# One layer of a hybrid SSD and convolution backbone: a new table of issue orders for the five engines

## The chip, the cores and the metric

The kernel runs on one core of a Trainium2 chip. The metric is the device time of one execution in microseconds (us). Five engines matter: TensorE (PE) does the matmuls, VectorE (DVE), ScalarE (ACT) and GpSimd (POOL) work on tiles element by element, and SyncE (SP) issues the DMAs. Each engine works through its own list of instructions in order; an instruction whose operand is not there yet holds up all that stands behind it on that engine.

## The reference

One layer of a diffusion backbone, for 512 latent tokens and 128 context tokens (640 columns in all, written T here), model width 1024. Cut to what matters:

```python
mod = silu(cond) @ w_ada + b_ada                      # six vectors of 1024, for latent and context
sh1, sc1, g1, sh2, sc2, g2 = split(mod, 6)
h = rms_norm(x, norm_mix_pre) * (1 + sc1) + sh1
z, xbc, dt_raw, cf_in = split(h @ w_in)
xbc = silu(dwconv1d(xbc, w_ssd_conv))                 # width 3
xs, b_mat, c_mat = split(xbc)
y_f, s_f = ssd_chunked(xs, dt_f, a_f, b_mat, c_mat, init_f)     # Mamba-2, chunks of 128, 16 heads
y_b, s_b = ssd_chunked(flip(xs), flip(dt_b), a_b, ...)          # and backward
y_ssd = rms_norm((y_f + flip(y_b) + xs * d_skip) * silu(z), ssd_norm)
u = cf_a * sigmoid(cf_g)                              # from cf_in
u = silu(layer_norm(dwconv1d(u, w_cf_conv)))          # width 31
mix = concat([y_ssd, u]) @ w_out
x = x + g1 * rms_norm(mix, norm_mix_post)
h = rms_norm(x, norm_ffn_pre) * (1 + sc2) + sh2
up = dwconv(h @ w_ffn_up)                             # 3x3 on latent tokens, width 3 on context
f = (silu(gate) * val) @ w_ffn_down                   # 2816 wide
x = x + g2 * rms_norm(f, norm_ffn_post)
```

Outputs are the new tokens and the final SSD states of the context. All is in float32.

## The kernel before

**Products.** Every tile has 128 channels on the partitions and the 640 tokens along the free axis. A float32 product is made as three products of reduced float32 (fp32r): weight and activation are split into a high part and the rest (hi and lo), and `mm3` (L408 to L414) adds hi·hi, hi·lo and lo·hi in PSUM, in two column halves of 384 and 256. A weight block of 128 by 1024 is called a unit: `fetch` (L286) has SP load it into `wr` (two buffers), `split_unit` (L290 to L312) has ACT copy the high part into `wh` (L310) and POOL (a few times DVE) subtract it to get `wl` (L312), three buffers each. Activations are split by `split_act` (L399, L401).

**Stages.** The times are those of the profile before.

- 0 to 36 us: x is loaded, squared on ACT (L497) and summed over channels on PE (L472, a product with ones, as every sum over channels); `rsqrt_mean` makes the root on ACT (L486) and its reciprocal on DVE (L487); `spread` (L480) brings it to all partitions. The first adaLN vectors are made by `ada_first` in four stages (L440 products of 16 loaded tiles, ACT copy L443, transpose L422, DVE L431), x is modulated (L522 to L533) and split, and the first three units run as the rows of h become ready. L506 is the product for dt.
- 36 to 340 us: projections, units 3 to 35, with eight pairs of heads p = 0 to 7 of the SSD between them. L657 to L664 prepare the decays. For each pair: transposes to tokens (L591), weighting by POOL (L729), chunk states (L743, L745) copied from PSUM by ACT (L747), the scan over chunks by POOL (L755, L758), state products y_off (L806, scaled by DVE L808), and the products within chunks y_diag (L817). The width-31 convolution runs on DVE (L871), some of its taps on ACT and POOL (L880, L884); ACT L851 is the gate's tanh.
- 340 to 400 us: the sums of the layer norm, the high and low parts of the first five SSD rows (L997 on DVE), the layer norm itself (DVE L980, ACT L984, DVE or POOL L985). Units 36 to 43, "ahead" parts of the output projection (the five SSD rows that need no layer norm), run beside it.
- 400 to 480 us: the rest of the output projection, units 44 to 58, and between its parts the remaining adaLN vectors, `ada_half` 0 to 5 (L459 products of eight tiles that SP has loaded into slots that the layer norm and the splits have read; then L462, L422).
- 480 to 535 us: class `Mid`, once for each column half: sum of squares and root, `spread`, `x2` (DVE L1155, L1157, ACT square L1158), `xsum` (L472), root, `spread`, and h2. Beside it units 59 to 64, the first up-projection units (L1258) and the last adaLN half, 6.
- From 535 us on: up-projections with the 3x3 convolution on DVE (L1236), down-projections, and the output.

**Order.** The program text makes the instructions in plain order; what is issued when is written out by hand in the table `ORDER`: for each engine the full sequence (PE 6677 entries, DVE 1076, ACT 785, POOL 412, SP 360) as ranges of program indices. `issue_in_order`, called at the end, ties each instruction to the one before it in that list, without a semaphore:

```python
for e, text in ORDER.items():
    order = []
    for word in text.split():
        a, _, b = word.partition("-")
        order += range(int(a), int(b or a) + 1)
    for a, b in zip(order, order[1:]):
        tc.add_manual_dep(given[e][b], given[e][a].name, behind, reason="order")
```

The buffers that an instruction uses and the data it waits for are fixed by the program text; the table sets only when it is issued on its engine.

Of the kernel before, what the change touches and what calls it, by code (L numbers as in the profile page):

```python
# [50 lines left out]
0-27 36-45 28-31 46-50 32-34 51-67 35 68-70 102 71-80 103 81-100 116-118 101 104-111 119-121 112-114 122  # L51
173-174 140-172 115 175-181 123-127 187-192 128-129 193-197 130-131 182-186 132-134 244-245 211-242 198
246-247 258-260 248-251 243 252 261-267 135-137 253 138-139 199-200 268-269 254-255 201-204 256-257 205-210
284-287 296-297 288-293 270 282-283 320-327 271-275 294-295 298 276 299-307 277 341 278-281 308-319 342-388
399-421 328-332 422-488 495-497 489-494 498-514 543-551 515-530 552-562 531-534 563-565 535-542 566-581
645-646 582-587 647-651 588 652-656 333-335 657-659 589-590 336-340 389-393 660-694 394-398 695-713 741-745
714-730 746-754 731-739 755-758 595 591-594 759-768 740 769-776 789-801 777-778 802-806 779-785 807-820
786-788 821-836 600-603 596-599 604-608 878-945 613-616 609-612 621-624 617-620 641-644 625-640 946-960
974-982 961 983-985 962 837-841 963 986 964-973 987-1018 1022-1023 1019-1021 1024-1033 846-849 842-845
854-857 850-853 1034-1043 1070-1078 1044-1058 1079-1084 1059-1069 1085-1107 1118-1129 1108-1117 1130 858-877  # L60
1131-1162 1207-1223 1163-1165 1224-1253 1255 1254 1256-1284 1303-1314 1285-1302 1315-1332 1351-1354
1333-1347 1166-1170 1355-1360 1348-1350 1361-1379 1450-1456 1380-1381 1457-1476 1382-1398 1175-1178
1171-1174 1183-1186 1179-1182 1203-1206 1187-1202 1477-1499 1399-1403 1500-1571 1594 1572-1589 1595-1601
1590-1593 1602-1608 1404-1408 1609-1622 1683 1623-1641 1409-1416 1421-1423 1417-1420 1424 1684-1715
1425-1437 1441-1444 1438-1440 1731-1746 1445-1449 1747-1755 1716-1720 1756-1758 1721-1724 1642-1646
# [12 lines left out]
2802-2809 2842 2854 2897-2901 2855-2860 2927-2930 2861-2873 2902-2924 2960-2962 2925-2926 2931-2935
2874-2886 2936-2938 2887-2892 2939-2958 2893 2959 3092-3093 2963-2975 3026 2976-2990 3027-3038 2991-2992
3039 3059-3070 2993-2998 3071 2999 3072-3073 3000-3016 3074-3077 3017-3024 3078-3090 3040-3044 3094-3096  # L80
3045-3058 3025 3097-3139 3158-3160 3140-3147 3161 3148-3157 3162 3203-3209 3163-3171 3210-3211 3172-3175
3184-3198 3212-3220 3301 3176-3183 3302-3306 3236 3199-3202 3091 3221-3235 3237-3245 3307-3310 3246-3253
3270 3311-3314 3271-3273 3315 3274 3316-3317 3275-3284 3318-3327 3332-3348 3254-3269 3285-3300 3328-3331
3380-3383 3349-3373 3388-3390 3397-3399 3410 3384-3387 3374-3376 3391-3393 3400-3402 3413-3415 3411
3406-3409 3539-3570 3412 3419 3422-3423 3420 3377-3379 3394-3395 3424 3431-3433 3440-3442 3449-3451 3421
3428-3430 3437-3439 3446-3447 3396 3403-3405 3448 3416-3417 3515-3517 3418 3518-3530 3425-3426 3531-3535
3455-3470 3477-3492 3471-3473 3536 3474-3476 3493-3499 3537 3427 3434-3436 3505-3508 3500-3504 3509-3514
3538 3443-3445 3452-3454 3572-3575 3644-3647 3668-3669 3576-3578 3648-3650 3670-3674 3579-3581 3571
3651-3653 3582-3584 3654-3656 3675-3680 3585-3587 3657-3659 3681-3682 3620-3623 3588-3590 3624-3625
# [12 lines left out]
419 395-400 420 428 401-403 432 463 404 464 405 465 442-443 406 421 423 444 424-425 407-409 422 445 410-412
# [1493 lines left out]
```

## Time and profile before

| | |
|---|---|
| median of 3 runs | 988.61 us (986.96 to 988.88) |
| the profiled execution | 989.1 us, of which the span 987.1 us |
| mean granted clock of PE over the span | 0.991 |
| busy: PE, DVE, ACT, POOL | 950.4, 690.3, 473.3, 577.1 us |
| moved by DMA | 117.52 MB, 119 GB/s on average |

The span runs from the first to the last instruction of the profiled execution; its time has 2.0 us besides. A row of the timeline reads: start in us, duration in us, engine, source line, operation, output <- input by the program's names, shape, type and count of instructions put together, and in brackets how long the engine had been idle before it and what it waited for. A row of the windows reads: stretch, its length, then for each engine the busy time and the count, then the mean granted clock of PE (1 is full speed), the busy share of the DMA engines and their GB/s.

### The profile page before, as it was taken

The page shows a single profiled execution, that of the slowest core. Times are in us where ns is not written, and L with a number is a line of the kernel's source. Part 1 is how long each engine was busy: PE and PEld are TensorE (multiplying, and loading weights), DVE is VectorE, ACT ScalarE, POOL GpSimd, SP SyncE. Part 2 cuts the span into 40 slices and gives each one's busy share as a digit, 9 for nine tenths or more (in the row PEclk, how much of TensorE's full clock was granted, in tenths as well). Part 3 has the DMA queues.
Part 4 walks back from the last instruction along what each step waited for, and adds up shares of the span by engine and source line. Part 5 has one row for each costly group of instructions (what it writes and reads, how often), then busy time and mean ns, then how long its engine had stood idle before and what let it go on. Part 6 is the DMA issues. An engine that isn't in the chain of part 4 may idle for free.

```text
span 987.1 us, 18794 instructions
## 1 busy us (share of the span) xinstructions
PE 950.4 (96%) x7623; PEld 925.3 (94%) x7623; DVE 690.3 (70%) x1076; ACT 473.3 (48%) x800; POOL 577.1 (58%) x416
## 2 busy tenths in 40 slices
PE   4999999999999999999989999999999999999995
PEld 2799999999999989999979999999999999999995
DVE  1769979999889997542674998999888898400004
ACT  4355756767578667723454843232332326322211
POOL 0344599989898862533752995444545446543444
PEclk9999999999999999999989999999999999999998
DMA  9721515335324532687662422222222221322213
GB/s 339 264 87 43 150 37 177 104 105 150 108 76 140 145 108 64 198 312 246 192 208 72 143 76 75 83 69 86 65 86 73 77 87 54 84 77 75 81 38 107
DMA packets 50294, 117.52 MB, mean 119 GB/s; under 512 B 6016, under 2 KB 13952, under 8 KB 50208
## 3 DMA queue, kind: packets, MB, share of 16 engines
q1 hardware_dynamic: 50208, 116.33, 36.6%
q8 instruction: 60, 0.98, 0.4%
q14 instruction: 26, 0.21, 0.1%
HBM read 112.55 MB, written 3.75 MB: 118 GB/s over the span
## 4 chain that ended last, share of the span: by engine, by line
PE 82%; DMA 6%; DVE 4%; ACT 3%; POOL 3%; issue 1%; SPq 1%; POOLq 0%; ACTq 0%; DVEq 0%
PE ps L414 68%; PE ps L1258 2%; PE pq L414 2%; PE pq L817 2%; PE pq L806 1%; POOL wl L312 1%; DMA T<-in_wada 1%; DMA wr<-in_wout 1%; PE pq L459 1%; DMA T<-in_xT 1%; PE pq L743 1%; DMA wr<-in_win 1%; PE pq L440 1%; DMA wr<-in_wrest 1%; ACT wh L310 1%
## 5 line engine op out<-in xcount | busy, mean ns | idle before, releaser
L312 POOL TENSOR_TENSOR wl<-wr,wh 128x1024 fp32r<-128x1024 f32 (+3 forms) x127 | 289.6, 2284 | 338.7 <-ACT wh L310 324.3
L414 PE MATMUL ps<-H,wh 128*128 128x384 f32 (+1 forms) x1636 | 314.6, 309 | 0.8 <-ACT u L851 0.5
L310 ACT ACTIVATE wh<-wr 128x1024 fp32r<-128x1024 f32 (+3 forms) x131 | 131.2, 1003 | 314.5 <-PE ps L414 202.2
L414 PE MATMUL ps<-T,wh 128*128 128x384 f32 (+1 forms) x1472 | 272.5, 306 | 1.8 <-ACT S L1226 1.8
L1236 DVE SCALAR_TENSOR_TENSOR S<-ps,prms,S 128x441 f32<-128x441 f32 (+2 forms) x336 | 233.5, 695 | 29.0 <-ACT S L1226 18.4
L414 PEld LDWEIGHTS ps<-H,wh 128*128 128x128 f32 x1636 | 248.7, 188 | 3.4 <-issue 1.9
L414 PEld LDWEIGHTS ps<-T,wh 128*128 128x128 f32 x1472 | 219.0, 188 | 2.2 <-ACT S L1226 2.1
L871 DVE SCALAR_TENSOR_TENSOR ps<-u,prms,ps 128x655 f32<-128x655 f32 x205 | 185.1, 903 | 11.9 <-ACT ps L868 6.6
L414 PE MATMUL ps<-H,wl 128*128 128x384 f32 (+1 forms) x818 | 190.3, 309 | 0.1
L414 PE MATMUL ps<-T,wl 128*128 128x384 f32 (+1 forms) x736 | 166.2, 306 | 0.0
L414 PEld LDWEIGHTS ps<-H,wl 128*128 128x128 f32 x818 | 128.2, 188 | 0.9 <-issue 0.5
L414 PEld LDWEIGHTS ps<-T,wl 128*128 128x128 f32 x736 | 113.1, 188 | 0.0
L487 DVE RECIPROCAL rsm<-rsm 128x160 f32<-128x160 f32 (+2 forms) x9 | 7.3, 817 | 148.2 <-ACT rsm L486 148.2
L414 PE MATMUL ps<-S,wh 128*128 128x384 f32 (+1 forms) x420 | 88.2, 311 | 0.0
L414 PEld LDWEIGHTS ps<-S,wh 128*128 128x128 f32 x420 | 67.6, 190 | 0.6 <-issue 0.2
L414 PE MATMUL ps<-S,wl 128*128 128x384 f32 (+1 forms) x210 | 55.8, 314 | 0.9 <-POOL wl L312 0.8
L788 ACT ACTIVATE S<-S,AC 128x128 f32<-128x128 f32 x140 | 46.6, 395 | 3.5 <-DMA S<-acD 3.5
L884 POOL TENSOR_TENSOR T<-T,T 128x640 f32<-128x640 f32 x20 | 33.2, 1659 | 20.6 <-ACT T L880 20.5
L414 PEld LDWEIGHTS ps<-S,wl 128*128 128x128 f32 x210 | 35.8, 190 | 2.0 <-POOL wl L312 1.3
L1226 ACT ACTIVATE S<-ps,prms 128x640 f32<-128x640 f32 x42 | 36.5, 868 | 0.0
L880 ACT ACTIVATE T<-u,prms 128x512 f32<-128x512 f32 (+1 forms) x54 | 28.5, 554 | 12.0 <-POOL T L884 9.7
L1338 POOL TENSOR_TENSOR H<-S,S 128x640 f32<-128x640 f32 x16 | 25.3, 1580 | 0.0
(346 smaller groups left out, 1195.9 us busy)
## 6 DMA issues: line engine op xcount, KB each, us to landing
wr<-in_wup SPq DMA_DIRECT2D x44, 512.0 KB, 3.5
wr<-in_win SPq DMA_DIRECT2D x36, 512.0 KB, 3.7
T<-in_wada SPq DMA_DIRECT2D x49, 256.0 KB, 5.7
S<-acD SPq DMA_DIRECT2D x28, 320.0 KB, 4.7
wr<-in_wdown SPq DMA_DIRECT2D x16, 512.0 KB, 3.5
wr<-in_wout SPq DMA_DIRECT2D x13, 512.0 KB, 4.2
H<-in_wada SPq DMA_DIRECT2D x23, 256.0 KB, 4.7
S<-in_wada SPq DMA_DIRECT2D x16, 256.0 KB, 4.4
```

The lines of the kernel that those rows point to most:

```text
L310: ac.activation(hi[:, :n], raw[:, :n], AF.Copy)
L312: lo_eng.tensor_tensor(lo[:, :n], raw[:, :n], hi[:, :n].bitcast(F32), SUB)
L414: last_mm[0] = te.matmul(out, w, x[:, c0:c1], start=first and i == 0, stop=last and i == 2)
L788: ac.activation(rc, rc, AF.Relu, scale=-1.0, bias=AC2[:, c, row:row + 1])
L817: te.matmul(py[64 * h:64 * h + 64, i * P:(i + 1) * P], xt[:, c * P + 64 * h:c * P + 64 * h + 64], rs[h, d][:, c * P:(c + 1) * P], start=d ...
L871: ve.scalar_tensor_tensor(acc, u[:, j:j + UO], w(j), acc, MUL, ADD)
L880: ac.activation(t[:, b:c], u[:, a:a + c - b], AF.Copy, scale=w(j))
L884: gp.tensor_tensor(far, far, t, ADD)
L1226: ac.activation(out, v, AF.Identity, bias=prm_col("ffn_b", i), scale=w(1, 1))
L1236: ve.scalar_tensor_tensor(ob, vl[:, r0 + a - 1:r1 + a - 1, q0 + b - 1:q1 + b - 1], w(a, b), ob, MUL, ADD)
L1258: te.matmul(pt[:, o:o + c1 - c0], w[k] if i in (1, 2) else w[:, k * P:(k + 1) * P], x[:, c0:c1], start=k == 0 and j == 0, stop=k == KD - 1 ...
L1338: gp.tensor_tensor(f_raw[q], a, b, MUL)
```

## The change

Only the table `ORDER` changes. All instructions, their operands, buffers and shapes stay. The entries stand at other places in the lists: 3297 of PE's (the first at place 28, now issued at 14.8 us, the last at place 3568, at 533.5 us), 475 of DVE's, 522 of ACT's, 224 of POOL's and 234 of SP's. Behind 535 us the five lists are the same. The head of PE's and the head of SP's list, as an example; the rest of the diff is more of the same kind:

```diff
 ORDER = {
     "PE": """
-0-27 36-45 28-31 46-50 32-34 51-67 35 68-70 102 71-80 103 81-100 116-118 101 104-111 119-121 112-114 122
-173-174 140-172 115 175-181 123-127 187-192 128-129 193-197 130-131 182-186 132-134 244-245 211-242 198
+0-31 36-49 32-34 50-53 35 54-90 104-105 102-103 91-101 116-119 106 120-126 107-115 127 187-191 175-180 192
+181-182 193 173-174 140-172 194-196 183-186 211-242 197-198 258-259 243 128-129 246-252 260-263 130-139
...
```

What is moved, as far as the lists show it at the places that the prediction speaks of (matmuls of PE between the one that starts a chain and the one that needs its result, before and after):

| place | before | after |
|---|---|---|
| start: place of the first weight load on SP's list | 25 | 19 |
| dt preparation, to L663 (99.3 us) | 5 | 36 |
| last product of a gate's unit, by ACT L851, to the next unit (119.7 us) | 8 | 18 |
| pair 3's states L745 to pair 2's y_off L806 (220.9 us) | 4 | 0 |
| pair 2's y_off L806, by DVE L808, to y_diag L817 (223.9 us) | 4 | 14 |
| pair 4's states L745 to pair 3's y_off L806 (253.5 us) | 0 | 4 |
| pair 7's tokens L591, by POOL L729, to states L743 (346.2 us) | 22 | 66 |
| last read of an H slot (unit 34) to the first ahead product that needs its new contents (348.4 us) | 97 | 12 |
| unit 62: last product that frees the low buffer, to its first low product (488.7 us) | 23 | 27 |
| first spread of half 0 to its column sums (497.9 us) | 114 | 123 |
| adaLN halves 0 and 1 | at about 425 us | right behind unit 44's first part |
| adaLN half 6 | at 511.8 us | 12 to 16 us later |

More of the change, by code (lines that the diff above doesn't have):

```diff
@@ L56 @@
[L56 to L65, printed above, removed]
@@ new lines @@
+1624-1626 1685-1700 1627-1641 1701-1718 1409-1432 1441-1442 1433-1435 1443-1444 1436-1440 1719-1723
+1731-1743 1724-1729 1744-1745 1730 1746-1755 1449 1445-1448 1756-1811 1827-1830 1812-1814 1642-1646
+1815-1823 1831-1835 1824-1826 1836-1866 1916 1867 1917-1918 1647-1682 1919 1868-1869 1920 1870-1874
+1921-2010 2012-2017 2011 2018-2022 1875-1879 2023-2080 2149-2150 2081-2089 2151-2157 2090-2103 2158-2164
+2104-2107 2165-2179 1884-1887 1880-1883 1892-1895 1888-1891 2197-2201 1912-1915 1896-1911 2202-2244
@@ new lines @@
+2640-2641 2659-2661 2642-2644 2693-2704 2616-2620 2669-2676 2705-2709 2662-2668 2717 2710-2711 2677-2682
+2712 2683-2686 2718-2727 2687-2689 2728 2713 2729-2740 2714 2690-2692 2830-2831 2771-2780 2832-2835
+2781-2790 2836-2841 2843 2741-2742 2715-2716 2792-2794 2743-2747 2791 2748-2755 2844-2847 2756-2758
+2795-2799 2848-2849 2800-2809 2850-2860 2894-2896 2960-2963 2897-2915 2964-2966 2916-2924 2967-2973
+2925-2926 2974-2987 2861-2892 2842 3092-3094 3026 2988-2990 3027-3035 2991-2992 3036-3045 3095 3046-3057
@@ new lines @@
+3624-3625 3591-3593 3596-3598 3594-3595 3599-3619 3626-3643 3660-3667 3683-4059 4061-4081 4060 4082-5548
+5597-5615 5549-5596 5616-5658 5693-5695 5659-5664 5696-5716 5665-5692 5717-6599 6665-6668 6600-6664
+6669-6676""",
+    "DVE": """
+0 3-4 1-2 13-16 18-19 17 5 20 11-12 23-26 6 27-30 7-9 21-22 33-35 38-39 36 10 37 31-32 41-42 46 43-44 40 47
+45 48 51 49 52 50 53-54 84-90 111-114 55-56 91-94 69 95-96 119-122 57-60 97-100 61-68 101-102 70-71 75
+123-125 103-106 72 152-155 76-77 82 78 73 107-109 79-80 74 81 110 83 126-129 163 130-135 115-118 136 156
@@ new lines @@
+529 532-533 538 531 535 524 540 534 557 536 539 517 541-543 545 544 558 546 548 550 547 559 552 560-561
+563-564 566 549 551 567 565 553 568 554-556 569 571-575 570 562 576-585 589 586-588 593 590 594 591-592 595
+597 596 598 601-602 599-600 605 603-604 606-612 615-616 613-614 617-749 1053 750-1046 1049-1051 1047-1048
+1052 1054-1063 1065 1064 1066-1075""",
+    "Activation": """
+0-3 7 6 4 8 5 9-11 15 18 12 19 17 21-22 13 20 24 23 25 35 26-27 32-33 14 30 28-29 16 48-49 47 31 56-58 61 64
+50-51 62 34 67 65-66 63 52-53 37-38 79 116 80 54 36 39 55 71 68 40-43 120 44-45 72 46 117 121-122 81 69-70
@@ new lines @@
+370 373-374 371 375-377 379 378 380-381 383 382 384-385 387 386 388-389 391 390 392-393 395 394 396-397 399
+398 400-411""",
+    "SP": """
+0-8 14 24 10 13 16 11 9 12 15 23 19 17 31 27 25 18 20 26 28-29 41 47 30 36 34-35 38 40 21 43 39 37 44-45 42
+46 48-49 22 50 32-33 53 52 54-57 72 81 51 59-61 82 58 64 62 83 63 87 96 68 67 97 65-66 69 98 75-76 74 70 73
+77 79-80 78 99 85 100 71 84 104 88-89 91 90 94-95 113 92 114 93 115 119 128 86 105 107 111-112 108 106 102
+129-130 109-110 134 143 101 120 122 121 123 126-127 124-125 103 116 118 144-145 149 135 158 137 141-142 117
```

173 lines of the change are left out of this document (78 added, 95 removed).

## The prediction

> **What bounds the kernel now.** I read the page first: busy shares, slices, clock.
>
> ```profile
> span 987.1 us, 18794 instructions
> PE 950.4 (96%) x7623; PEld 925.3 (94%) x7623; DVE 690.3 (70%) x1076; ACT 473.3 (48%) x800; POOL 577.1 (58%) x416
> PE   4999999999999999999989999999999999999995
> PEclk9999999999999999999989999999999999999998
> ```
>
> TensorE (PE) is busy 96% of the span, and the change leaves its 6677 instructions as they are, only in another order. So what can be won is PE's idle time, the time at a reduced clock, and little else. The windows show where that lies (columns: sum and count per engine, then granted clock, DMA share, GB/s):
>
> ```profile
> core 0: us, PE busy (x) PEld busy (x) DVE busy (x) ACT busy (x) POOL busy (x), PEclk, DMA share, GB/s
> 0.00:36.50 36.50, 21.77 (x294) 14.51 (x295) 14.19 (x28) 14.30 (x22) 5.80 (x17) 0.95 0.96 348
> ...
> 95.00:340.00 245.00, 242.14 (x1856) 238.31 (x1855) 222.18 (x301) 167.22 (x341) 215.21 (x185) 1.00 0.39 116
> 340.00:350.00 10.00, 8.60 (x98) 7.45 (x98) 9.18 (x9) 10.00 (x24) 9.02 (x7) 1.00 0.64 217
> 350.00:435.00 85.00, 84.88 (x794) 81.01 (x793) 55.45 (x84) 51.70 (x80) 38.15 (x33) 1.00 0.44 143
> 435.00:480.00 45.00, 44.17 (x475) 41.78 (x474) 17.38 (x23) 15.37 (x24) 19.55 (x13) 1.00 0.79 271
> 480.00:494.50 14.50, 13.55 (x124) 12.57 (x125) 10.49 (x19) 7.66 (x15) 11.97 (x9) 1.00 0.48 154
> 494.50:505.20 10.70, 7.59 (x96) 6.61 (x96) 6.92 (x10) 5.55 (x10) 5.99 (x5) 0.68 0.54 172
> 505.20:535.00 29.80, 28.85 (x289) 27.38 (x289) 17.55 (x49) 13.07 (x32) 12.09 (x8) 1.00 0.42 142
> 535.00:987.10 452.10, 440.32 (x3155) 438.96 (x3153) 293.62 (x480) 158.13 (x217) 237.15 (x131) 0.99 0.25 80
> ```
>
> From 535 us on, the five old and new lists are the same (the last place that differs is PE's 3568th, at 533.5 us), so the last 452 us stay. Before that PE is idle 36.50 − 21.77 = 14.73 us in the start, and 2.86 + 1.40 + 0.12 + 0.83 + 0.95 + 3.11 + 0.95 = 10.2 us after it (36.5 to 95 has none). Those 25 us are all that is at stake, with the half clock near 500 us. The marks of PE in the timeline (start, duration, then idle before and what released it) say what the 10.2 us are:
>
> ```profile
> 99.30 0.28 PE L663 MATMUL pq<-csts,T 128*32 128x128 f32 x1 [0.27 <-ACT CDs L657]
> 119.67 0.73 PE L414 MATMUL ps<-H,wh 128*128 128x384 f32 x3 [0.49 <-ACT u L851]
> 223.86 0.55 PE L817 MATMUL pq<-S,S 128*64 128x128 f32 x6 [0.33 <-DVE S L808]
> 252.89 0.60 ACT L747 ACTIVATE AT<-pq 128x512 f32<-128x512 f32 x1 [0.30 <-PE pq L745]
> 253.54 0.71 PE L806 MATMUL pq<-M,S 128*128 128x128 f32 x4 [0.69 <-ACT AT L747]
> 346.23 0.49 PE L743 MATMUL pq<-S,M 128*128 128x128 f32 x2 [1.24 <-POOL S L729]
> 348.42 0.86 PE L414 MATMUL ps<-H,wh 128*128 128x384 f32 x4 [0.16 <-DVE H L997]
> 488.68 0.39 PE L414 MATMUL ps<-S,wl 128*128 128x256 f32 x1 [0.83 <-POOL wl L312]
> 495.37 0.87 PE L472 MATMUL pq<-T,ones 128*32 128x96 f32 x32 [0.21 <-ACT T L1158]
> 497.89 0.37 PE L472 MATMUL pq<-T,ones 128*32 128x96 f32 x8 [1.65 <-ACT T L1158]
> 499.50 2.02 PE L480 MATMUL pq<-rsm,csts 128*128 128x96 f32 x8 [1.25 <-DVE gs L1125]
> 513.53 1.30 PE L459 MATMUL pq<-S,cts 128*32 128x128 f32 x40 [0.84 <-DMA S<-in_wada]
> ```
>
> Each is PE coming to a matmul whose operand another engine has not finished. A wait costs somewhat more than its mark, since a record includes the pipelined end of its last matmul: three matmuls after a wait take 0.73, four 0.86, so one adds 0.13 and the fixed part is 0.34; I add 0.15 per mark.
>
> **The change, part by part.** Nothing is added or removed, so I counted, along the old and the new lists, how many matmuls PE has between the one that starts a chain and the one that needs its result. In a full stretch a matmul takes:
>
> ```profile
> 620.00:640.00 20.00, 20.00 (x141) 20.00 (x140) 18.47 (x33) 6.13 (x7) 9.72 (x5) 1.00 0.22 71
> ```
>
> 20.00 / 141 = 0.142 us; in 480 to 494.5, where columns are halved, 13.55 / 124 = 0.109.
>
> *Start.*
>
> ```profile
> 12.86 1.36 ACT L497 ACTIVATE S<-T 128x640 f32<-128x640 f32 x2 [1.46 <-PE pq L472]
> 13.65 0.33 SPq L245 DMA_DIRECT2D S<-in_wada  x1
> 16.92 0.39 ACT L486 ACTIVATE rsm<-pq,epsc 128x160 f32<-128x160 f32 x1 [2.70 <-PE pq L472]
> 17.05 0.89 SPq L286 DMA_DIRECT2D wr<-in_win  x2
> 33.03 0.62 PE L506 MATMUL pq<-T,wdts 128*32 128x512 f32 x2 [0.84 <-DVE T L533]
> ```
>
> The DMA is 96% busy here, so a load moved up pushes others back. The first weight load goes up six places on SP's queue, to where a load now issues at 13.65 instead of 17.05: unit 0's split, and with it PE's first projection matmuls (L414), can come 3 us sooner. The squares on ACT run in another sequence (that of x's fourth chunk behind four others); one 0.7 us square late delays the rsqrt by 0 to 0.7, I take 0.35. Of the first adaLN loads, those of the second stage come later; following their landings by hand, its modulation comes 1.9 us later, the third stage's 3.8 us earlier, and PE has the 3 us of projection work to fill in. At the end of the four stages I get PE 1.0 us ahead; bounds −2.0 (the 3 us less 1.0) to +1.5 (the 1.9 less 0.4 uncovered). Term: −1.0.
>
> *95 to 435 us, waits that go.* L663 (99.30): 5 matmuls between before, 36 after, 5 us for ACT's 0.57. Tanh to gate (119.67): 8 becomes 18, 2.6 us. L747 to L806 (253.54): none becomes 4 matmuls of L743, 0.9 us against the 0.6 + 0.3 that the chain takes. POOL's weighting of pair 7's tokens (346.23): 22 matmuls become 66, 8 us. First ahead matmul's 0.16 too, but see below. With 223.86 (4 becomes 14) and small marks of 0.39 in all: 0.27 + 0.49 + 0.33 + 0.69 + 0.39 + 1.24 + 0.16 = 3.57, and ten marks by 0.15: −5.1.
>
> *New waits there.* Pair 3's states (L745, 219.8 us now) and pair 2's y_off (L806), which writes the same PSUM tile, had 4 matmuls between them and now stand side by side: the 0.60 of L747 and about 0.3 around it, +0.85 (between 0.69, the mark at 253.54 where PE had the same adjacency, and 1.0). In pair 6, y_off (L806) to y_diag (L817) has 0.44 us of cover instead of 0.89 where DVE's L808 ran just in time: +0.5 (0 to 0.9). The first ahead matmul moves up: 12 matmuls, 1.7 us, instead of 97 ahead of a DVE split (L997) that must itself wait until that slot's last projection has read it: +0.6 (0.16 now, to 1.5). Sum +1.95; the term is −3.1.
>
> *435 to 480 us and the adaLN halves.* Most halves get 3 to 19 us more between load and use, which takes the waits for L422 (0.83 idle in all here) and their ends, −1.1. But halves 0 and 1 are asked for some 20 us earlier, right behind unit 44's first part, while the buffers they load into are still being read by the layer norm:
>
> ```profile
> 391.91 5.94 DVE L980 TENSOR_TENSOR T<-T,ps 128x640 f32<-128x640 f32 x8 [1.45 <-PE ps L480]
> 398.30 1.58 POOL L985 TENSOR_TENSOR S<-T,H 128x640 fp32r<-128x640 f32 x1 [1.00 <-ACT T L984]
> 399.93 1.58 DVE L985 TENSOR_TENSOR S<-T,S 128x640 fp32r<-128x640 f32 x2 [1.03 <-POOL S L985]
> T<-in_wada SPq DMA_DIRECT2D x49, 256.0 KB, 5.7
> H<-in_wada SPq DMA_DIRECT2D x23, 256.0 KB, 4.7
> ```
>
> POOL's L985 ends 399.88 − 391.91 = 8 us after the spread; with 4.7 to 5.7 for the load, data is there 12.7 to 13.7 us after it. PE gets there in 98 matmuls, between 98 × 0.107 (84.88 / 794) = 10.5 and 98 × 0.142 = 13.9. Stall 0 to 3.2; I take +0.8, from a mix of the two kinds of matmul, 12.5 us, against the middle of the data's times, 13.2. Half 5's load now stands behind a weight load on SP: +0.5 (0 to 1.5). The term: +0.2.
>
> *480 to 494.5 us.* Unit 62's low part (488.68) gets 27 instead of 23 matmuls of cover: 4 × 0.109 = −0.4; the other 0.4 of the mark stays.
>
> *494.5 to 505.2 us.* The x2 chain of half 0 (spread, DVE, ACT squares, column sums) has 123 instead of 114 matmuls inside: 9 × 0.109 = −1.0 of the 0.21 + 1.65. The spread of 499.50 keeps its 1.25: between column sums and spread stand no matmuls in either list. The clock there:
>
> ```profile
> 498.40:505.20 6.80, 5.70 (x31) 5.36 (x32) 4.29 (x9) 3.82 (x6) 2.63 (x2) 0.50 0.53 179
> ```
>
> Half clock for 6.8 us, in which 5.70 of busy time would be 2.85 at full. I leave it in, since the two longest marks stay close together, and keep −2.85 as a bound. [...]
>
> *505.2 to 535 us.* Half 6 (L459, 513.53) moves 12 to 16 us later, far behind its loads if these land like the two rows above: 0.84 and the end, −1.1 with a small mark beside it.
>
> *Sum.* −1.0 − 3.1 + 0.2 − 0.4 − 1.0 − 1.1 = −6.4. Distances count only PE's side: at 346.23 PE had 22 matmuls of cover and still stood 1.24, because POOL was late with its own queue. DVE, ACT, POOL and SP are reordered too (475, 522, 224 and 234 places), and waits that this makes are not among my pairs. Of the old order's 10.2 us, 3.3 (a third) lies in such queue-made waits by my reading of the marks above (POOL L729 1.24, POOL wl 0.83, DVE gs 1.25); I put back a third of the gain, +2.1. Net −4.3. The profiled execution took 989.1 (span 987.1 and 2.0 around it): 984.8; it is 0.5 above the median 988.61, so 984.3.
>
> **Rivals.** *Waits only move.* The new list's unseen waits eat the whole 6.4: 988.6 by the median, anything from 987 to 990. For it speaks that where the mark at 223.86 goes, one of the same kind comes a few matmuls earlier; against, that the 346.23 and 513.53 marks have 6 us and more of new cover.
>
> *Slower: POOL late with weights.* One mechanism: from 95 to 340 us, POOL is busy 215.2 of 245 us (88%) and DVE 222.2 (91%), and the new list gives PE its state products (L743) 5 to 14 us later against the projections. If POOL's splits (L312) then stand behind weight products (L729), each late low part costs what 488.68 shows, 0.83 + 0.15 = 0.98. One in each of the eight pairs gives 984.3 + 8 × 0.98 = 992.1; it decides from the fifth on (4.3 / 0.98 = 4.4). Against: in 95 to 340 no mark of PE names POOL wl today.
>
> [...]
>
> **How the numbers follow.** This kernel's runs spread by 0.2% (986.96 to 988.88), about 2 us, and that is what a measurement can tell from no change. Chances: forecast (982.5 to 986.6) 0.50; full clock 0.13; waits only move 0.22; slower 0.15. Faster: 0.50 + 0.13 = 0.63, same 0.22, slower 0.15. Range: down to 980 (full clock and the start's −2.0 bound, with some of the put-back not needed), up to 990, which takes in the moved waits; what is left out is most of the 0.15 above and a little below.
>
> **What would show it.** Right: PE idle in 95 to 435 falls from 4.4 to 2 or 3; no marks at L663, at pair 3's y_off, at pair 7's first L743, or by half 6's load; new marks at pair 2's y_off from ACT L747, at the first ahead matmul from DVE L997, and at L459 near 405 us from the loads of wada; the stretch from 535 us on as long as now. [...] Wrong: marks from POOL wl between 95 and 340, over 16 us of PE idle in the first 50 us, or a stall at 405 us of over 3 us.

## The result, and the profile after

The new table is faster: 981.87 us (median of 6 runs, 980.44 to 984.74) against 988.26 us (6 runs, 986.96 to 989.44), a ratio of 0.9933 with a 95% interval of 0.9919 to 0.9947, so 5.2 to 8.0 us. The forecast was 984.3 us. The profiled execution took 981.19 us, 979.4 of it the span. All lines are one higher than before (L415 was L414); in the edited kernels of the experiments they are two lower than before (L412 was L414).

The engines' row of the page after:

```profile
PE 944.5 (96%) x7623; PEld 920.9 (94%) x7623; DVE 686.9 (70%) x1076; ACT 471.3 (48%) x799; POOL 577.9 (59%) x416
```

PE has the same 7623 matmuls in 944.5 us instead of 950.4. Of the 7.7 us by which the span shrank, 5.9 are thus busy time and 1.8 idle time: most of the gain is not in the marks. A matmul record grows at half clock: the eight of the spread took 2.02 us at 499.50 before and take 1.13 at 494.92 after. The two half-clock stretches of the trace before, 3.4 us in the start and 6.8 near 500, are up to 1.7 + 2.85 = 4.55 of the 5.9; what the rest is isn't shown. The windows after:

```profile
0.00:36.50 36.50, 22.70 (x307) 16.10 (x309) 15.40 (x28) 15.27 (x22) 7.56 (x18) 1.00 0.99 362
36.50:95.00 58.50, 58.06 (x481) 56.43 (x472) 43.84 (x81) 30.31 (x43) 21.89 (x14) 1.00 0.25 81
95.00:340.00 245.00, 242.81 (x1857) 239.55 (x1856) 223.71 (x302) 165.32 (x335) 214.48 (x186) 1.00 0.39 117
340.00:350.00 10.00, 10.00 (x113) 9.51 (x112) 9.49 (x15) 9.36 (x24) 7.88 (x8) 1.00 0.66 201
350.00:435.00 85.00, 83.70 (x778) 79.07 (x777) 52.54 (x75) 52.49 (x83) 39.24 (x31) 1.00 0.45 146
435.00:480.00 45.00, 42.85 (x488) 39.80 (x487) 14.50 (x28) 15.87 (x26) 22.27 (x14) 1.00 0.80 272
480.00:494.50 14.50, 11.80 (x147) 11.05 (x145) 10.15 (x17) 7.93 (x16) 11.70 (x8) 1.00 0.54 171
494.50:505.20 10.70, 10.19 (x80) 9.20 (x81) 9.30 (x20) 6.15 (x11) 7.94 (x5) 1.00 0.62 198
505.20:535.00 29.80, 29.80 (x307) 28.94 (x306) 19.29 (x58) 14.12 (x37) 7.62 (x7) 1.00 0.41 140
535.00:979.40 444.40, 432.57 (x3090) 431.21 (x3088) 288.70 (x459) 154.53 (x208) 237.32 (x131) 0.99 0.26 80
498.40:505.20 6.80, 6.71 (x53) 5.72 (x52) 6.58 (x14) 3.66 (x7) 4.48 (x2) 1.00 0.74 229
```

Read length minus PE busy: idle time fell from 14.73 to 13.80 us in the start, from 2.86 to 2.19 in 95 to 340, from 1.40 to none in 340 to 350, from 3.11 to 0.51 in 494.5 to 505.2 and from 0.95 to none behind it; it grew from none to 0.44 in 36.5 to 95, from 0.12 to 1.30 in 350 to 435, from 0.83 to 2.15 in 435 to 480 and from 0.95 to 2.70 in 480 to 494.5. The last row is the stretch that ran at 0.50 before; now its clock is 1.00. Behind 535 us the idle time is as before (11.83 against 11.78 us).

The timeline after, PE's marks (start, duration, in brackets the idle time and what ended it), then the ACT and SP rows behind two of them:

```profile
132.53 0.77 PE L592 MATMUL pq<-csts,S 128*128 128x128 f32 x5 [0.69 <-ACT AT L748]
172.12 0.91 PE L807 MATMUL pq<-M,S 128*128 128x128 f32 x6 [0.73 <-ACT AT L748]
217.78 0.94 PE L807 MATMUL pq<-M,AT 128*128 128x128 f32 x6 [0.69 <-ACT S L748]
399.97 1.30 PE L460 MATMUL pq<-H,cts 128*32 128x128 f32 x40 [0.98 <-ACT AT L1030]
454.70 0.97 PE L460 MATMUL pq<-T,cts 128*32 128x128 f32 x24 [0.74 <-DMA T<-in_wada]
455.88 0.43 PE L460 MATMUL pq<-T,cts 128*32 128x128 f32 x8 [0.21 <-DMA T<-in_wada]
457.34 0.52 PE L460 MATMUL pq<-T,cts 128*32 128x128 f32 x10 [1.03 <-DMA T<-in_wada]
483.45 0.50 PE L415 MATMUL ps<-S,wh 128*128 128x256 f32 x2 [1.59 <-ACT wh L311]
486.01 0.39 PE L415 MATMUL ps<-S,wl 128*128 128x256 f32 x1 [0.28 <-POOL wl L313]
494.92 1.13 PE L481 MATMUL pq<-rsm,csts 128*128 128x96 f32 x8 [1.25 <-DVE gs L1127]
542.49 0.82 PE L415 MATMUL ps<-T,wh 128*128 128x384 f32 x4 [1.76 <-ACT S L1227]
...
394.27 0.42 SPq L749 DMA_DIRECT2D out_nsb<-S  x1
398.67 0.92 ACT L985 ACTIVATE S<-T,prms 128x640 fp32r<-128x640 f32 x1 [1.78 <-DMA out_nsb<-S]
447.09 0.33 SPq L287 DMA_DIRECT2D wr<-in_wrest  x1
451.28 0.53 ACT L311 ACTIVATE wh<-wr 128x384 fp32r<-128x384 f32 x1 [2.49 <-PE ps L415]
```

Gone are the marks at L663, at the gate's unit (119.67), at pair 3's y_off (253.54), at pair 2's y_diag (223.86), at pair 7's tokens and at half 6's loads, and in the x2 chain (497.89) both 1.65 and 0.21. New are those at pair 1's and pair 2's y_off (172.12 and 217.78), at adaLN loads (399.97 and 454 to 458) and at the high part of unit 62 (483.45). The mark at 132.53, of transposes (L592), is not new: the same transposes waited 0.69 at 131.29 before.

**How much is clock.** One minus the mean granted clock, times the span, is the time lost to it: 0.0080 × 987.4 = 7.9 us on the mean of 67 runs of the kernel before, 0.0058 × 980.4 = 5.7 us on 12 runs of the new one (6 of them those of the repeat below); three disturbed executions of 1580 to 2419 us are left out of means and ratios throughout. Among the runs of one and the same kernel, 1 us more of it goes with 0.86 us more time (179 runs, each against its kernel's mean). The two means are 989.42 and 982.45 us, 7.0 apart (5.8 in the first set of runs, 7.1 in the repeat); of that 0.86 × 2.2 = 1.9 is clock and about 5.1 the order. The two profiled executions lie further apart in clock (0.991 and 0.996, so 8.9 and 3.9 us lost): of their 7.9 us about 4.3 is clock and 3.6 the order. The order is thus worth 3.6 to 5.1 us.

**Where the order gains.** Since PE's instructions are the same but in another sequence, I gave each kind of matmul its usual spacing, summed this along either list, and compared the times at which the two traces reach equal sums:

| time before, us | lead of the new one, us |
|---|---|
| 31.6 | 1.0 |
| 54.8 | 2.7 |
| 95.3 | 3.2 |
| 149.3 | 5.0 |
| 220.0 | 2.4 |
| 334.3 | 3.8 |
| 381.9 | 6.2 |
| 416.6 | 3.9 |
| 457.8 | 5.3 |
| 492.8 | 2.3 |
| 516.4 | 8.2 |
| 531.8 and later | 7.8 |

So the start gives 3.2, 95 to 382 gives 3.0, 382 to 493 takes 3.9 back, and 493 to 532 gives 5.5. Where the sequences differ most, the rows are rough: with kinds told apart by line and shape, 416.6, 457.8 and 516.4 come out at 2.5, 8.9 and 9.6, while 381.9, 492.8 and 531.8 stay within 0.1. Part of the first and the last stage is clock: up to 2.85 of the last, by the prediction's row for 498.4 to 505.2 us and the row above. The window of the kernel before that shows the part in the start:

```profile
24.00:27.40 3.40, 3.40 (x35) 1.55 (x35) 3.36 (x7) 2.98 (x4) 1.96 (x1) 0.51 1.06 393
```

3.4 us at half clock while PE has 35 matmuls to do; this trace of the new kernel has no such stretch there. But the order does not decide it: the repeat of the new kernel below has one (25.5 to 28.9 us), and a version with the old start (old_fill) has none. So up to 1.7 of the 3.2 is chance of these two executions.

### The profile page after: what moved, and what is told of

It is laid out like the page before. It is cut to its first block, busy times and chain, and to the rows that moved or that the text cites. A ratio compares the mean times of both kernels' runs of the same rounds, so it can differ in the third digit from the quotient of the medians.

```text
span 979.4 us, 18795 instructions
## 1 busy us (share of the span) xinstructions
PE 944.5 (96%) x7623; PEld 920.9 (94%) x7623; DVE 686.9 (70%) x1076; ACT 471.3 (48%) x799; POOL 577.9 (59%) x416
## 4 chain that ended last, share of the span: by engine, by line
PE 87%; DMA 3%; ACT 3%; DVE 2%; SPq 1%; POOL 1%; issue 1%; POOLq 0%; ACTq 0%; DVEq 0%
PE ps L415 72%; PE ps L1259 3%; PE pq L415 2%; PE pq L818 2%; PE pq L807 1%; PE pq L460 1%; SPq L452 1%; DMA wr<-in_wout 1%; PE pq L744 1%; PE pq L441 1%; POOL wl L313 1%; PE pq L473 1%; DMA S<-acD 1%; ACT wh L311 1%; DMA T<-in_wada 1%
## 5 line engine op out<-in xcount | busy, mean ns | idle before, releaser
L415 PE MATMUL ps<-H,wh 128*128 128x384 f32 (+1 forms) x1636 | 315.7, 309 | 0.1
L415 PE MATMUL ps<-T,wh 128*128 128x384 f32 (+1 forms) x1472 | 272.5, 306 | 1.8 <-ACT S L1227 1.8
L415 PEld LDWEIGHTS ps<-H,wh 128*128 128x128 f32 x1636 | 249.0, 188 | 2.7 <-issue 1.7
L415 PEld LDWEIGHTS ps<-T,wh 128*128 128x128 f32 x1472 | 218.9, 188 | 2.2 <-ACT S L1227 2.1
L415 PE MATMUL ps<-H,wl 128*128 128x384 f32 (+1 forms) x818 | 191.8, 309 | 0.0
L415 PE MATMUL ps<-T,wl 128*128 128x384 f32 (+1 forms) x736 | 166.2, 305 | 0.0
L415 PEld LDWEIGHTS ps<-H,wl 128*128 128x128 f32 x818 | 129.0, 188 | 1.0 <-issue 1.0
L415 PEld LDWEIGHTS ps<-T,wl 128*128 128x128 f32 x736 | 113.0, 188 | 0.0
L415 PE MATMUL ps<-S,wh 128*128 128x384 f32 (+1 forms) x420 | 88.0, 310 | 1.6 <-ACT wh L311 1.6
L415 PEld LDWEIGHTS ps<-S,wh 128*128 128x128 f32 x420 | 66.5, 188 | 2.8 <-ACT wh L311 1.8
L415 PE MATMUL ps<-S,wl 128*128 128x384 f32 (+1 forms) x210 | 54.9, 309 | 0.3 <-POOL wl L313 0.3
L1227 ACT ACTIVATE S<-ps,prms 128x640 f32<-128x640 f32 x42 | 36.5, 869 | 0.0
L415 PEld LDWEIGHTS ps<-S,wl 128*128 128x128 f32 x210 | 35.2, 188 | 0.9 <-POOL wl L313 0.5
```

What stands on the lines that cost most here:

```text
L415: last_mm[0] = te.matmul(out, w, x[:, c0:c1], start=first and i == 0, stop=last and i == 2)
L1227: ac.activation(out, v, AF.Identity, bias=prm_col("ffn_b", i), scale=w(1, 1))
```

## The experiments

All medians are in us; ratios are to the kernel before, run beside each (989.4 to 989.7 us there).

**The repeat.** The new kernel again, unedited:

```diff
 (no edit)
```

> The new kernel itself, once more beside the old one. If its gain is order (4 us less waiting) plus clock (3 us less lost at half clock), the granted clocks of its runs average 0.994 to 0.995 against 0.991 to 0.992 of the old one, and the ratio is 0.993 again. If the clock's part was chance, the clocks agree and the ratio is 0.996.

982.63 (980.62 to 984.34), ratio 0.9927 (0.9912 to 0.9942), with a mean clock of 0.9938 against 0.9920. The gain repeats, and so does the better clock. The trace shows something else: the wait behind 535 us, which both orders have (mark 1.76). The timeline before and of the repeat (the row after stands above):

```profile
550.24 0.83 PE L414 MATMUL ps<-T,wh 128*128 128x384 f32 x4 [1.76 <-ACT S L1226]
```

```profile
544.16 1.29 PE L415 MATMUL ps<-T,wh 128*128 128x384 f32 x4 [1.76 <-ACT S L1227]
```

And the window from 535 to 565 us, first after, then the repeat:

```profile
535.00:565.00 30.00, 28.24 (x204) 28.06 (x203) 27.78 (x45) 24.67 (x38) 29.62 (x21) 1.00 0.40 131
```

```profile
535.00:565.00 30.00, 28.24 (x197) 28.06 (x196) 26.18 (x43) 23.77 (x36) 27.95 (x20) 0.94 0.40 136
```

The same wait of 1.76 us is followed by a half-clock stretch in one execution (four matmuls take 1.29 us instead of 0.82, clock 0.94 over 30 us) and not in the other. Equal busy time holds 7 matmuls less, some 1 us. One kernel's runs spread by this much.

The traces show what differs. The starts of the half-clock stretches of one trace lie whole multiples of 3.413 us apart (23.92, 498.38 and 979.66 in the trace before: 139 and 141 steps; 25.47 and 544.29 in the repeat: 152), and the stretch at 23.92 is one such step long. Windows of 3.413 us, counted from these starts (in the trace after from its one, 971.90), around this wait, first after (two), then the repeat (one):

```profile
538.41:541.82 3.41, 2.32 (x20) 2.12 (x18) 3.27 (x6) 3.41 (x8) 3.33 (x3) 1.00 0.74 225
541.82:545.23 3.41, 2.74 (x18) 2.77 (x19) 3.22 (x6) 3.41 (x6) 3.41 (x4) 1.00 0.84 311
```

```profile
540.88:544.29 3.41, 1.65 (x14) 1.47 (x13) 3.22 (x7) 3.41 (x8) 3.33 (x4) 1.00 0.70 266
```

After, a boundary cuts the wait in two, and PE is busy 0.68 and 0.80 of either window; in the repeat the whole wait falls into one window, PE is busy 0.48 of it, and the next window runs at half clock. In the traces before and after, from 17.1 and 19.6 to 970 us and without the half-clock windows themselves, none of the 551 windows in which PE was busy 0.62 or more was followed by half clock; of the three others, those of 0.42 (494.96) and 0.56 (20.51), both before, were, and the one of 0.53 (480.38 after) was not.

**The start: one list's, then the other's.** Each engine's list up to what one order issues before a time, then what is left in the sequence of the other.

```diff
 ORDER, all five engines                       # start_new
-old list
+new list's entries issued before 84 us, then the rest as in the old list

 ORDER, all five engines                       # start_old
-new list
+old list's entries issued before 87 us, then the rest as in the new list
```

> All that the new lists issue in their first 84 us stands first, in the new order; everything else follows in the old order. Theory (the gain adds up by stages: -3.2 us in the start, -3.1 from 95 to 370, +2.5 to +3.5 in the adaLN halves, -4.9 near 500 us with the clock): about 3.2 less than before, 985.1. Rival (a start that ends earlier is given back at the next wait for a loaded or split operand): 987.5 to 988.5.

> The old order for the first 87 us, the new order for all the rest. Theory by stages: 3.2 more than the new kernel, 985.1. Rival (given back): 981.9 to 982.5, the start does not matter.

The new start alone: 987.72, ratio 0.9981 (0.9968 to 0.9993), so 1.9 us faster, 0.7 to 3.2. The old start before the new rest: 987.09, ratio 0.9977 (0.9961 to 0.9993), and 0.47% or 4.6 us over the new kernel, 3.1 to 6.2 by this version's interval alone and more with the new kernel's own. Both hold the 3.2 of the traces only at an edge, and the first lies between theory (3.2) and rival (0 to 0.8). With 1.9 and 4.6 they show that the start is worth something and is not all given back later; their middle is 3.2, but neither alone measures that.

**The middle: the cut at 477 and at 382 us.**

```diff
 ORDER, all five engines                       # chain_new
-new list
+old list's entries issued before 477 us, then the rest as in the new list

 ORDER, all five engines                       # to382_new
-old list
+new list's entries issued before 382 us, then the rest as in the old list
```

> The old order up to 477 us, then the new order. Theory by stages with the clock: the granted clock stays at 1.00 from 490 to 510 us and the time falls by about 5 to 983.3. Rival (order alone, the clock's dip comes at random): the dip near 500 us is there again and the time falls by 2.0 to 2.5, to 986.

> The new order up to 382 us, then the old one. Theory by stages: the start and the projections keep their 6.2, the dip near 500 us comes back as in the old order, so 988.3 - 6.2 = 982.1, near the new kernel though its last stages are the old ones. Rival (given back later): 985 to 988.

Both missed: 988.68, ratio 0.9995 (0.9981 to 1.0008), and 989.66, ratio 0.9994 (0.9976 to 1.0013). The timelines show why. In the first:

```profile
479.22 0.37 PE L470 MATMUL pq<-msq,ones 128*32 128x96 f32 x8 [1.91 <-POOL msq L1076]
...
493.21 0.36 PE L412 MATMUL ps<-S,wh 128*128 128x256 f32 x1 [1.14 <-DVE M L1069]
```

and in the second, timeline and one window:

```profile
385.03 0.48 PE L470 MATMUL pq<-HL,ones 128*32 128x160 f32 x8 [0.74 <-ACT HL L834]
387.92 1.35 PE L478 MATMUL ps<-rsm,csts 128*128 128x160 f32 x8 [1.87 <-DVE rsm L485]
```

```profile
490.00:510.00 20.00, 16.93 (x182) 15.12 (x181) 11.61 (x22) 11.59 (x22) 11.87 (x7) 0.83 0.66 215
```

At the seam, five lists that were not made for each other meet: chains that either order covers stand bare, 1.91 + 1.14 = 3.05 us in the first, 2.61 in the second, in which the lead is 5.8 us ahead of the seam and 2.6 behind it. The second also has the half clock near 500 us again (0.83 over 20 us). So has the first in its profiled execution, a shorter one from 502.0 to 505.4 us, against its theory of a clock of 1.00 there:

```profile
490.00:510.00 20.00, 16.94 (x178) 15.36 (x178) 14.02 (x26) 11.73 (x23) 12.24 (x9) 0.91 0.54 171
```

The mean clock of its runs is still better (0.9938 against 0.9916 for the kernel before beside it). A list cut in a stage of short chains is no clean test of either half. So what 95 to 382, 382 to 493 and 493 to 532 us are worth rests on the two traces and is not shown by an experiment.

**The three waits for a state's copy.** At 172.12 and 217.78 matmuls of y_off, at 132.53 five transposes, wait for ACT's copy of a state that PE has just made. Projection products are put between:

```diff
 ORDER["PE"]                                   # new_swaps
-603 608 604-607 926-931 917-923 932
+603 917-923 608 604-607 926-931 932
-1111 1112-1117 846-849 842-845 854-857
+1111 846-849 842-845 1112-1117 854-857
-1171-1178 1183-1186 1179-1182 1471-1476 1477
+1171-1178 1471-1476 1183-1186 1179-1182 1477
```

> The new order with three moves on PE alone: six or seven projection matmuls put between a pair's last L745 and the product that waits for ACT L747, at the three places where the new trace has marks of 0.69, 0.73 and 0.69. Theory (each new wait lies on the path and costs its mark and 0.15): 2.6 less than the new kernel. Rival (the waits move to the next split or to POOL): 0 to 0.8 less.

978.87 (977.81 to 981.44, 5 runs), ratio 0.9898 (0.9882 to 0.9914), 2.8 us below the new kernel by the means, 3.0 and 3.8 by the medians of its two sets of runs. The marks at 132.53 and 217.78 are gone. At 172 us PE still waits:

```profile
170.38 0.89 ACT L562 ACTIVATE M<-ps,prms 128x640 f32<-128x640 f32 x1 [0.78 <-PE ps L412]
171.85 0.91 PE L804 MATMUL pq<-M,S 128*128 128x128 f32 x6 [1.51 <-issue]
```

ACT's L562 stands ahead of the state's copy in ACT's list and waits for the end of a projection tile, and the moved matmuls are that end: they delay the ACT they were to cover. Two of three waits of some 0.7 us with their ends would be 2 × (0.69 + 0.15) = 1.7, the better clock of these runs (0.9950 against 0.9942) 0.7. But the third wait grew from 0.73 (1.43 in the repeat) to 1.51, and PE's idle time from 95 to 340 us is 1.60, against 2.19 after and 2.80 in the repeat: idle time accounts for 0.6 to 1.2. So the size of the theory (2.6) was met partly by luck, and a part of the gain stays unexplained.

**The adaLN loads.** Two loads move up on SP's list, to before the store and the weight loads that they stood behind; the second makes eight loads of T go ahead of a weight load (246):

```diff
 ORDER["SP"]                                   # new_ada
-147 161 172 ... 184 162 194
+147 161 162 172 ... 184 194
-219 212 246 209 223-225 218 220-222 247
+219 212 209 223-225 218 220-222 246 247
```

> The new order with two moves on SP alone: the weight load of unit 55, which stood 4.3 us for its buffer with eight adaLN loads behind it, goes behind those loads; the store of pair 7's state, for whose landing ACT's L985 and so the first adaLN half waited, goes to where its twin is issued, 27 us earlier. Theory (SP's queue made the marks of 0.98 at 400 us and 0.74 + 0.21 + 1.03 near 455 us): those marks go, 3.5 less than the new kernel. Rival (the loads come late because the DMA engines are full there, 0.94 to 1.00 busy): no more than 1 less, with marks of the same size.

983.41, ratio 0.9943 (0.9923 to 0.9963): not faster than the new kernel. Its timeline:

```profile
401.00 0.42 PE L457 MATMUL pq<-T,cts 128*32 128x128 f32 x8 [0.20 <-DMA T<-in_wada]
...
447.58 0.33 SPq L284 DMA_DIRECT2D wr<-in_wrest  x1
...
453.06 0.52 ACT L308 ACTIVATE wh<-wr 128x384 fp32r<-128x384 f32 x1 [6.04 <-DMA wr<-in_wrest]
453.63 0.44 PE L412 MATMUL ps<-S,wh 128*128 128x384 f32 x1 [2.91 <-ACT wh L308]
```

The mark of 0.98 at 400 is gone (one of 0.20, for a load, is left behind it), so its cause was the store that moved: a store of a state (`out_nsb`, issued at 394.27 after) had to read its buffer before ACT's layer norm might write it, and ACT stood 1.78 for it (398.67); here, and in new_best below with the same move, that ACT instruction starts without a wait. ACT L1030, which the mark names, only stood behind. The three waits for T (0.74 + 0.21 + 1.03 = 1.98) went too, but the weight unit, issued 0.5 us later than after and behind eight loads, is not there when ACT wants it: its high part starts at 453.06, waiting for the load, instead of 451.28, where it waited for PE, and PE stands 2.91 for it. The DMA is 0.80 busy from 435 to 480 us after; the loads share it, and SP's order decides here which of the two PE waits for. The mean clock of these runs is 0.9927 against 0.9942, worth 1.3 us, so apart from the clock this version is about even: what the T loads and the store give, the weight unit takes. The clock is not apart from the order, though: the wait of 2.91 has a half-clock stretch behind it (454.6 to 458.0 us). By the time the rival was right (no gain), by the mechanism neither: the marks went, and another came.

Both edits together:

```diff
 ORDER                                         # new_all
+the three moves of new_swaps on PE
+the two moves of new_ada on SP
```

> All five moves. Theory: the two gains add, 6 less than the new kernel, 976. Rival: 979 to 982.

982.97, ratio 0.9933 (0.9919 to 0.9947). The swaps' 3 us do not show. The mean clock, 0.9927 against 0.9950 for the swaps alone, takes 0.86 × 2.3 = 2.0 of them; the trace has the weight unit's wait again (3.02) with half clock behind it (453.7 to 457.1). The rest goes with the loads, as far as the version before shows it.

**The clock near 500 us.** In the new list, put matmuls from inside the chain behind it, so that its waits come close together again; in the old list, spread matmuls from elsewhere into the chain, so that its two waits break up:

```diff
 ORDER["PE"]                                   # new_gap
-3332-3337 3339-3348 3254-3269 3285-3300 3328-3331 3349
+3332-3337 3254-3269 3285-3300 3328-3331 3339-3348 3349

 ORDER["PE"]                                   # old_fill (the old list)
-3285-3300 3328-3331 3380-3383 3349-3373
+3285-3296 3349-3356 3297-3300 3357-3367 3328-3331 3380-3383 3368-3373
```

> The new order with ten matmuls of units 63 and 64, which stand right ahead of half 0's column sums, put behind the spread that follows. PE comes to the sums 1.2 us too early and stands there, as it did in the old order, besides the 1.25 ahead of the spread. Theory (PE's clock is halved for 3.4 us or more after any few us that hold some 2 us or more of waiting): the clock near 495 to 505 us falls to half in nearly every run, the mean granted clock falls by 0.002 to 0.003, and the time rises by 1.2 for the waiting and 1.7 to 2.9 for the clock, 2.9 to 4.1 over the new kernel. [...]

> The old order with one edit on PE: eight matmuls of unit 64 put ahead of the last column sum of half 0 and eleven ahead of the spread, so that the marks of 1.65 and 1.25 near 498 us are filled as far as unit 64's low part is ready. Theory: 1.9 us less waiting, and the half clock from 498.4 to 505.2 is gone in most runs, 1.7 to 2.9 more: 3.6 to 4.8 less than the old kernel, 985. Rival (the clock dips there whatever PE does, or the waiting moves on to the up-projection): 1.9 or less, 987 to 988.5.

The first: 989.6, ratio 1.0001 (0.9984 to 1.0019), some 7 us over the new kernel. Its timeline and a window:

```profile
496.39 0.95 PE L470 MATMUL pq<-T,ones 128*32 128x96 f32 x24 [0.99 <-ACT T L1156]
497.94 0.79 PE L470 MATMUL pq<-T,ones 128*32 128x96 f32 x24 [0.59 <-ACT T L1156]
499.97 1.93 PE L478 MATMUL pq<-rsm,csts 128*128 128x96 f32 x8 [1.25 <-DVE rsm L485]
...
511.00 1.01 PE L1256 MATMUL ps<-T,wh 128*128 128x384 f32 x2 [2.13 <-ACT wh L308]
```

```profile
500.00:503.50 3.50, 3.50 (x17) 3.50 (x18) 1.83 (x4) 1.29 (x4) 3.25 (x3) 0.51 0.02 5
```

With 0.99 + 0.59 + 1.25 within 5 us the half clock is back, one stretch of 3.5 us, and eight spread matmuls take 1.93 us instead of 1.13. That fits the theory. The rest of the 7 us was not expected: a unit's high part is 2.13 us late at 511 us, and a second half-clock stretch, of 6.8 us, begins in that wait (510.3 to 517.2). That the moved matmuls free the buffers for which this unit waits is my reading of the list, not shown by a run. The profiled execution is also one of the slowest (994.09) and has further stretches at 25.6 and 175.8 us, where nothing was edited. Over all runs the mean clock, 0.9905 against 0.9942, is worth 3.1 us and the wait as forecast 1.2; some 3 us more are not accounted for.

The second: 987.38, ratio 0.998 (0.9968 to 0.9992), 2.0 us faster than the old list, which is the rival's figure (1.9 or less) and not the theory's. Timeline and window:

```profile
496.68 0.39 PE L412 MATMUL ps<-S,wl 128*128 128x256 f32 x1 [0.68 <-POOL wl L310]
501.94 0.44 PE L1256 MATMUL ps<-T,wh 128*128 128x384 f32 x1 [0.55 <-ACT T L1175]
502.87 0.44 PE L1256 MATMUL ps<-T,wh 128*128 128x384 f32 x1 [0.49 <-DVE T L1180]
504.17 0.45 PE L1256 MATMUL ps<-T,wh 128*128 128x384 f32 x1 [0.51 <-DVE T L1180]
505.67 0.44 PE L1256 MATMUL ps<-T,wh 128*128 128x384 f32 x1 [0.36 <-ACT T L1175]
511.63 1.30 PE L457 MATMUL pq<-S,cts 128*32 128x128 f32 x40 [1.17 <-DMA S<-in_wada]
```

```profile
498.40:505.20 6.80, 5.25 (x39) 4.08 (x38) 5.38 (x12) 4.46 (x8) 3.53 (x2) 1.00 0.72 251
```

The waits are not less: the chain runs sooner, and PE now waits for the rows of h2 behind it (0.55 + 0.49 + 0.51 + 0.36) and longer for half 6's load (1.17 against 0.84). But from 496 to 506 us they come in pieces of 0.7 us at most with work between, and the clock stays at 1.00. The theory's dip is thus gone in this trace, but its saving of waits is not there, and the mean clock of the runs, 0.9939 against 0.9927 beside them, is worth only 1.0 of the 2.0 us; where the other 1.0 comes from isn't shown. The two kernels bracket the half clock at 500 us in one trace each: with the waits bunched it comes, with waits in pieces it does not. The busy share says the same: the least that PE is busy in any 3.41 us between 490 and 512 us is 0.15 in the trace before, 0.54 in this one and 0.63 after.

**The wait behind 535 us.** In the new list, the 3x3 convolution's row comes one step sooner:

```diff
 ORDER                                         # new_tail
 PE
-3620-3623 3588-3590 3624-3625 3591-3593 3596-3598 3594-3595 3599
+3588-3595 3620-3625 3596-3598 3599
 ACT
-581 579
+579 581
```

> The new order with one edit behind its changed part: nine matmuls of other tiles go behind the last ones of unit 67's tile, and ACT makes that tile's first convolution step (L1226 in the old numbering) ahead of a weight copy instead of behind it. That is for the mark of 1.76 near 541 us, the same in both orders, after which some traces show half clock for 3.4 us and others do not. Theory: the mark goes, 1.9 less, and with it the dips it sets off in part of the runs, 0.8 on the mean: 2.0 to 2.7 less than the new kernel. Rival: DVE's convolution, which holds the tile, is late all the same: 0 to 0.8 less.

982.76 (979.33 to 988.2), ratio 0.9931 (0.9903 to 0.9958): no change against the new kernel is seen, though with runs so far apart (2.7 us either way) one of 2 us could hide. The wait moved to the next chain:

```profile
549.66 0.82 PE L412 MATMUL ps<-T,wh 128*128 128x384 f32 x4 [1.31 <-ACT U L1302]
```

1.76 became 1.31, so by the trace 0.4 is won of an expected 2, as the rival had it.

**What helped, together.**

```diff
 ORDER                                         # new_best
+the three moves of new_swaps on PE
+the store's move of new_ada (147 161 162 172 ... 184 194) on SP
+the moves of new_tail on PE and ACT
```

> The new order with the three moves on PE that took 2.9 us away (projection matmuls behind the last L745 of a pair), with the store of pair 7's state issued 27 us earlier on SP, and with the edit for the mark of 1.76. If the parts add: 2.9 + 0.6 + 2.3 = 5.8 less than the new kernel, 976.5 to 977. If one eats another: 978 to 980.

979.42 (977.99 to 984.14), ratio 0.9903 (0.9883 to 0.9923): some 9 us below the kernel before and 2.3 below the new one by the means, whose two intervals (0.9919 to 0.9947 and 0.9912 to 0.9942) overlap this one at its upper edge. It is the same as the swaps alone (0.9898), so the parts do not add; the swaps remain the simplest version below both.

## Why the prediction was right, point by point

- **Sign and size.** Forecast −4.3 from the order with the half clock kept; measured −7.0 on the means, the order −3.6 to −5.1, the clock the rest. So the order's sum was right in size, but the time was not: 981.87 lies in the range, outside the forecast's own 982.5 to 986.6, and nearest to the full clock that was given 0.13 (984.3 less the 2.85 of the prediction's row, 981.5). The step that failed there is the half clock that I left in at 498.4 to 505.2 us because the two longest marks would stay close together: one of them, 1.65, went, and the clock is 1.00 in that stretch. On average 1.9, two thirds of the 2.85, went, since a half-clock stretch can still come elsewhere, as behind the 1.76 wait behind 535 us in the repeat (0.94 over 30 us). That the order's sum comes out is partly luck, as the terms below show.
- **Start, −1.0.** Low: 3.2 in the traces, with 1.9 and 4.6 by the swapped starts. The prediction had no term for the half clock in the start; a stretch of 3.4 us at 0.51 is up to 1.7 of it, which leaves the order −1.5 or more, inside its bounds, and that this stretch is in the one trace and not in the other is chance.
- **95 to 435 us, −3.1.** The lead grew by 3.0 from 95 to 382, so the size holds there. Of its parts, the five waits went as said, though the list of marks left out one of 0.69 at 131.29, which stays (132.53); pair 2's y_off came (0.69 against 0.85). Two waits it named did not come (first ahead product +0.6, pair 6's y_diag +0.5), and one that it did not see came at pair 1's y_off (0.73 at 172.12). PE's idle time fell from 4.4 to 3.5, not to 2 or 3.
- **435 to 480 us, +0.2, and unit 62, −0.4: the step that failed.** From 382 to 493 the new order loses 3.9. Of the 0.83 of idle time that the term ascribed to L422, only 0.37 was L422's; the other marks stood before L459, for loads. The stall at halves 0 and 1 was right in size (0.98 at 400 against 0.8) by luck, since it was wrong in cause: not POOL's and DVE's layer norm but a store issued at 394.27 that ACT waited for. Nor are both halves asked for 20 us earlier: one runs at 399.97, the other only at 420.26 (both about 425.8 before). The half that paid was another one: I gave half 5 +0.5, and halves 3 and 4 wait 1.98 at 454 to 458. There I followed PE's distances and not the order in which the loads share the DMA. And unit 62's low part did fall from 0.83 to 0.28, somewhat more than counted, but its high part now stands 1.59. No other load shared the DMA with that one: SP stood 3.3 us until POOL's subtraction (476.97 to 478.79) had freed the `wr` buffer, and ACT then waited 1.96 for it to land. So here it is the pace of the splits. PE's idle time by the windows grew by 4.25 from 350 to 494.5 us, which roughly fits the 3.9.
- **x2 chain, −1.0, and half 6, −1.1.** Here 5.5 was won, up to 2.85 of it clock. The whole 1.86 of the x2 marks went and not 1.0, but not by the nine more matmuls alone: between spread and sums PE now spends 13.7 us instead of 11.4; the matmuls are 1.0 of that, and the waits inside at unit 62, 1.87 instead of 0.83, the rest. The wait for ACT's square is gone because PE waits for weights meanwhile. Part of this gain is thus the loss of the stage ahead, seen again. The spread's 1.25 stayed (494.92), as said, and half 6's mark went.
- **The put-back, +2.1.** From 382 to 532 us the terms summed to +0.2 − 0.4 − 1.0 − 1.1 = −2.3 with the half clock kept. The lead grew by 1.6 there, up to 2.85 of it clock, so the order lost up to 1.25, and up to 3.5 had to be put back. The sign of the put-back was right, its size low; it was spread over all stages by the prediction, and sat in this one.
- **The rivals.** POOL late with weights: no mark of PE names POOL's low parts between 95 and 340 us after either; it fell. Waits only move: true from 382 to 493, not over all.
- **The clock.** The 2.85 is worked out from the prediction's row; whether shorter waits would leave full clock there was my estimate, and no run had shown it. What the runs showed: a stretch of half clock lasted 3.4 us (500.0 to 503.5 at 0.51 in new_gap) or 6.8 (498.4 to 505.2 before), and ahead of it came waits of 0.99 + 0.59 + 1.25 (new_gap), a single 3.02 (new_all) or a single 1.76 (the repeat). The 1.76 had both outcomes: half clock behind it in the repeat, with PE busy 0.48 of the window that held it (544.16), and none after, with 0.68 and 0.80 of the two that it fell into (542.49).

What stays open: why the wait at 172 us varies from 0.73 to 2.16 us between kernels that do not differ there, how the order's gain in the start divides among its moves, and, since neither cut in the middle was clean, whether the loss from 382 to 493 us and the gain behind it hold by themselves.

## What to carry to other kernels

When only an order changes, compare the two traces at equal work done and not at equal time: that showed a stage that lost 3.9 us inside a gain of 7. Count distances on the DMA queue too and not on PE alone: where loads are 0.8 of the time busy, shuffling the loads moved a wait and did not remove it, while three groups of matmuls put between a state and its first use went with 2.8 us, though only two of them removed their wait. Break up bunched waits of PE even if their sum stays: near 500 us PE was busy at least 0.54 of any 3.41 us with the waits in pieces and 0.15 with them bunched, and half clock came in the second, in one trace each (old_fill and before).

## What the hardware showed that I had not expected

- Up to 970 us half clock came in stretches of 3.4 us or twice that, behind waits of 1.76 us (544.16 in the repeat), or of 0.99 + 0.59 + 1.25 within 5 us (new_gap), while waits of 1.25 alone (494.92) and 1.59 alone (483.45) had none in the trace after, and waits in pieces of up to 0.68 had none (old_fill). Counted in windows of 3.413 us from the starts of these stretches, it came behind those in which PE was busy 0.42 and 0.56 (before) and 0.48 (the repeat), but not behind one of 0.53 (after), and behind none of the 551 of 0.62 or more (before and after). A stretch costs 1.0 us by the matmuls missing from the repeat's window (7 × 0.142), and at most half its length, 1.7.
- The same 1.76 wait, in the same kernel, had it in one execution (a window busy 0.48) and not in another (two windows busy 0.68 and 0.80), so two runs of one kernel can differ by 1 us or more with no change of order.
- A small store that is late on the queue can hold up a later writer of its buffer: 1.78 us of ACT (398.67) for a store of a state, seen as 0.98 of PE two steps on.
